# Attention with ropes from SBUF copies, normalisation in the output's evacuation, and transposes one slot later

## The chip, the cores and the metric

The kernel runs on one core of one Trainium2 chip. The metric is the device time of one execution in microseconds (us), the median of several executions. The engines are TensorE (PE in the rows, its weight loads PEld), VectorE (DVE), ScalarE (ACT), GpSimd (POOL) and SyncE (SP), which issues the loads of the weights. SBUF is the on-chip memory that all engines read; PSUM holds TensorE's results.

## What is computed

One layer of a hybrid encoder over 256 tokens of width 2048, with 16 learned meta tokens ahead of them (272 positions). Cut to what matters here:

```python
h = rms_norm(x); aq, ak, av, mk, mq, mv, mo, gates = split(h @ w_in)
# A) differential attention, 8 heads, two components of 64 each
q = rope(aq) * 64 ** -0.5;  k = rope(ak)           # rope on the first 16 of each 64
p = softmax(q @ k.T)                                # for each of two components c
a = p[c=0] - lam * p[c=1]
o_attn = head_rms(a @ av) * gain
# B) bidirectional mLSTM, 4 heads, on mk, mq, mv; gated by sigmoid(mo)
o_ml = head_rms(mlstm(conv(mk), conv(mq), mv)) * gain * sigmoid(mo)
x = x + concat(o_attn, o_ml) @ w_out                # "wo"
x = x + swiglu_ffn(rms_norm(x));  out = rms_norm(x) # gate, up, down
```

## The kernel before, in words

**Stages of TensorE.** Each projection stage computes 512 columns of weights against all tokens: `aq0 ak0 av0 aq1 ak1 av1 mk mq mv0 mv1 mo0 mo1`, then `wo0` to `wo3`, then the FFN. A stage (`project`, L216) has four PSUM accumulators `acc_<stage>_0` to `_3`, and takes the 16 blocks of the inner dimension in 8 pieces of two blocks (`wh_av0_3` is piece 3 of av0). Each product is three matmuls, high by high, high by low, low by high (L251 to L253). The pieces go in pairs: for pieces (0, 1) all four accumulators in turn, 12 matmuls each, then pieces (2, 3), and so on, 48 matmuls for a pair of pieces. A piece's high part is made by ScalarE (`wh`, L205) and its low part by VectorE (`wl`, L206, one instruction for each of the two blocks; in `wo` one for a piece, L213). The PSUM pool holds four accumulators, so the next stage's accumulator j has to wait until this stage's accumulator j has been read.

**Reading the accumulators.** Of aq0 and of av and mv, ScalarE copies each accumulator to an SBUF tile (`value_copy`, L607, `vt_...`, five buffers). Of aq1, ak0 and ak1 the rope itself reads PSUM: a shuffle (L815) and a product (L818) on VectorE, issued with high priority and, but for the first shuffle, pinned to the written order; then a product and a sum on GpSimd (L819, L820).

**Attention** runs beside the projections as a generator that is advanced once for every second piece, a *slot*. For head h and block b of 128 queries, `scores` makes `pss{h}{b}` on TensorE, the row maximum (L860) and its scaling (L861) on VectorE, two exponentials with row sums on ScalarE (L863), then on VectorE the reciprocal (L867), the product with -lambda (L868), the scaled first component (L869) and the difference of both (L870). `transposes` (`pat`, L877) comes one slot after `scores`, `values` (`po`) later, and `finish` writes `om`. `stack` (L829) prepares `qs`, `ks` and `klow` for a head.

**mLSTM.** It runs in the same slots after attention: its last step transposes the normalised heads (`pht{h}{half}`, L804) and ScalarE scales them into `hT` (L807). GpSimd multiplies them with the gate (L977) and subtracts the high part (`split_mix`, L827), which gives `mixh` and `mixl`; `mixh12` to `mixl15` are the last two blocks' worth of pieces, 6 and 7, of `wo`. Behind these GpSimd adds the residual `res` (L990), to which VectorE adds the accumulators of wo (L1000).

**What sets the order.** A scheduler works out one order for each engine ahead of time from the program and its own estimate of times; each engine then runs its list in that order and waits where an operand is late. So an edit in attention moves instructions on all engines, far behind attention too.

Of the kernel before, what the change touches and what calls it, by code (L numbers as in the profile page):

```python
# [86 lines left out]
def tile_hybrid_encoder_layer(  # L87
# [42 lines left out]
    def f(ap):  # L130
        return ap.bitcast(F32)
# [677 lines left out]
    def rope(ps, t0, name, first=False):  # L809
        n = NT - t0  # L810
        dst = kpool.tile([P, n], F32, tag="qk", bufs=32, name=name)
        sh = mp.tile([P, NT], F32, tag="ev", bufs=4, name=f"sh_{name}")
        swap = list(range(8, 16)) + list(range(8)) + list(range(16, 32))
        with tc.high_priority():
            shuffle = V.stream_shuffle(sh[:, :n], ps[:, :n], swap)  # L815
            if not first:
                pin(shuffle)
            pin(V.tensor_tensor(dst, ps[:, :n], ropeC[:, t0:], ALU.mult))  # L818
        G.tensor_tensor(sh[:, :n], sh[:, :n], ropeS[:, t0:], ALU.mult)  # L819
        G.tensor_tensor(dst, dst, sh[:, :n], ALU.add)  # L820
        return dst
# [7 lines left out]
    def attention(h0, nh):  # L829
        es, at, hs, on, qs, ks = {}, {}, {}, {}, {}, {}  # L830

        def stack(h):
            q, k = aq[h], ak[h]
            qs[h] = mp.tile([P, 2, SEQ], F32R, tag="qs", bufs=2, name=f"qs{h}")
            ks[h] = mp.tile([P, 2, NT], F32R, tag="ks", bufs=2, name=f"ks{h}")
            kz = klow[h % 2]
            for c in range(2):
                own, other = slice(64 * c, 64 * c + 64), slice(64 - 64 * c, 128 - 64 * c)
                A.copy(qs[h][own, c, :], q[own])
                A.copy(ks[h][own, c, :], k[own])  # L840
                A.copy(ks[h][other, c, :], k[own])
                V.tensor_tensor(qs[h][other, c, :], q[own], f(qs[h][own, c, :]), ALU.subtract)
                V.tensor_tensor(kz[own, c, :], k[own], f(ks[h][own, c, :]), ALU.subtract)
# [7 lines left out]
        def scores(h, b):  # L851
# [9 lines left out]
            V.tensor_scalar(st[:, 0:2], st[:, 0:2], QK_SCALE, None, ALU.mult)  # L861
            for c in range(2):
                A.activation(  # L863
                    e[:, c, :], pss[:, c, :NT], AF.Exp, bias=st[:, c:c + 1], scale=QK_SCALE,
                    accum_out=st[:, 2 + c:3 + c],
                )
            V.reciprocal(st[:, 4:6], st[:, 2:4])  # L867
            V.tensor_tensor(st[:, 5:6], st[:, 5:6], nlam, ALU.mult)  # L868
            V.tensor_scalar(e[:, 0, :], e[:, 0, :], st[:, 4:5], None, ALU.mult)  # L869
# [13 lines left out]
        def values(h):  # L883
# [10 lines left out]
            A.copy(on[h], po[:, :SEQ].rearrange("p (b d) -> p b d", d=P))  # L894
# [21 lines left out]
        for t in range(n + 3):  # L916
            if t % 2 == 0 and t + 2 < n:
                stack(h0 + t // 2 + 1)
            if t < n:
                scores(h0 + t // 2, t % 2)  # L920
            if 1 <= t <= n:
                transposes(h0 + (t - 1) // 2, (t - 1) % 2)
            if t >= 3 and t % 2:
                values(h0 + (t - 3) // 2)
            if t >= 6 and (t - 6) % 4 == 0:
                finish(h0 + (t - 6) // 2)
                finish(h0 + (t - 6) // 2 + 1)
            if t < n + 2:
                yield
        attending.remove(h0)  # L930

    for g in range(2):
        if g:
            accs = in_proj(C_AQ + N_CHUNK, NM, "aq1")
        if g == 0:
            accs = value_copy(accs, "q0", SEQ)
        for j in range(4):
            aq[4 * g + j] = rope(accs[j], NM, f"aq_{4 * g + j}", g and j == 0)
# [3 lines left out]
        accs = in_proj(C_AK + g * N_CHUNK, 0, f"ak{g}", pre=() if g else pre, pins=0 if g else 4)  # L942
        for j in range(4):
            ak[4 * g + j] = rope(accs[j], 0, f"ak_{4 * g + j}", j == 0)
# [245 lines left out]
```

## Time and profile before

| | |
|---|---|
| median of 3 executions | 1133.64 us (1133.54 to 1134.06) |
| profiled execution | 1134.18 us, of which the span of the engines 1132.3 us |
| TensorE busy | 1114.3 us (98%) |
| VectorE, ScalarE, GpSimd busy | 730.0, 649.6 and 244.5 us |

The span is that of the profiled execution, from its first to its last instruction; 1.9 us of its time lie around it. Busy times add up an engine's instructions. An engine that is 98% busy over the whole span can still wait in a few stages, and these are to be looked for by stretch.

### The profile page before, as it was taken

The page shows a single profiled execution, that of the slowest core. Times are in us where ns is not written, and L with a number is a line of the kernel's source. Part 1 is how long each engine was busy: PE and PEld are TensorE (multiplying, and loading weights), DVE is VectorE, ACT ScalarE, POOL GpSimd, SP SyncE. Part 2 cuts the span into 40 slices and gives each one's busy share as a digit, 9 for nine tenths or more (in the row PEclk, how much of TensorE's full clock was granted, in tenths as well). Part 3 has the DMA queues.
Part 4 walks back from the last instruction along what each step waited for, and adds up shares of the span by engine and source line. Part 5 has one row for each costly group of instructions (what it writes and reads, how often), then busy time and mean ns, then how long its engine had stood idle before and what let it go on. Part 6 is the DMA issues. An engine that isn't in the chain of part 4 may idle for free.

```text
span 1132.3 us, 19840 instructions
## 1 busy us (share of the span) xinstructions
PE 1114.3 (98%) x7629; PEld 1043.5 (92%) x7629; DVE 730.0 (64%) x1153; ACT 649.6 (57%) x1179; POOL 244.5 (22%) x315
## 2 busy tenths in 40 slices
PE   9999999999999999999999999999999999999996
PEld 8889999999999999999999999999999888888896
DVE  6886986998766758566556566556655645454544
ACT  6567688778976445555455555545554644444443
POOL 7320220021045923222122122122122100000000
PEclk9999999999999999999999999999999999999998
DMA  8556446554445666566566576676666765666563
GB/s 258 177 147 185 136 136 181 153 159 142 148 151 185 197 204 194 187 211 199 186 220 190 187 225 191 189 231 189 190 222 189 253 202 200 202 197 203 192 204 109
DMA packets 112255, 212.85 MB, mean 188 GB/s; under 512 B 8906, under 2 KB 9744, under 8 KB 112016
## 3 DMA queue, kind: packets, MB, share of 16 engines
q1 hardware_dynamic: 111664, 210.48, 59.5%
q8 instruction: 60, 0.98, 0.3%
q10 hardware_dynamic: 176, 1.06, 0.3%
q14 instruction: 35, 0.29, 0.1%
q0 software_dynamic: 320, 0.04, 0.0%
HBM read 209.45 MB, written 2.10 MB: 187 GB/s over the span
## 4 chain that ended last, share of the span: by engine, by line
PE 91%; DVE 5%; DMA 2%; issue 1%; ACT 1%; SPq 0%; POOL 0%; ACTq 0%; DVEq 0%; POOLq 0%
PE acc_up L248 14%; PE acc_ga L248 14%; PE acc_ga L249 7%; PE acc_up L249 7%; PE acc_dn L1086 7%; PE acc_dn L1083 7%; PE acc_dn L1087 7%; PE acc_wo L251 3%; PE acc_wo L252 3%; PE acc_wo L253 3%; PE acc_mv L251 1%; PE acc_mv L252 1%; PE acc_mv L253 1%; PE acc_mo L253 1%; PE acc_mo L251 1%; PE acc_mo L252 1%
## 5 line engine op out<-in xcount | busy, mean ns | idle before, releaser
L248 PE MATMUL acc_ga<-vhl,wh_ga 128*128 128x512 f32 x704 | 227.4, 382 | 0.0
L248 PE MATMUL acc_up<-vhl,wh_up 128*128 128x512 f32 x704 | 227.0, 382 | 0.0
L213 DVE TENSOR_TENSOR wl_dn<-raw_dn,wh_dn 128x1024 fp32r<-128x1024 f32 x88 | 108.5, 1234 | 115.5 <-ACT wh_dn L212 115.5
L249 PE MATMUL acc_ga<-vhl,wl_ga 128*128 128x256 f32 x704 | 182.1, 273 | 0.0
L249 PE MATMUL acc_up<-vhl,wl_up 128*128 128x256 f32 x704 | 181.6, 273 | 0.0
L213 DVE TENSOR_TENSOR wl_up<-raw_up,wh_up 128x1024 fp32r<-128x1024 f32 x88 | 114.8, 1335 | 79.8 <-ACT wh_up L212 79.8
L212 ACT CAST wh_dn<-raw_dn 128x1024 fp32r<-128x1024 f32 x88 | 92.3, 1050 | 125.9 <-PE acc_dn L1087 115.8
L213 DVE TENSOR_TENSOR wl_ga<-raw_ga,wh_ga 128x1024 fp32r<-128x1024 f32 x88 | 105.3, 1227 | 68.1 <-ACT wh_ga L212 68.1
L248 PEld LDWEIGHTS acc_ga<-vhl,wh_ga 128*128 128x128 f32 x704 | 130.8, 189 | 16.4
L248 PEld LDWEIGHTS acc_up<-vhl,wh_up 128*128 128x128 f32 x704 | 130.8, 189 | 16.3
L1083 PE MATMUL acc_dn<-wh_dn,ffh 128*128 128x512 f32 (+1 forms) x396 | 141.2, 357 | 0.0
L1087 PE MATMUL acc_dn<-wh_dn,ffl 128*128 128x512 f32 (+1 forms) x396 | 141.2, 357 | 0.0
L1086 PE MATMUL acc_dn<-wl_dn,ffh 128*128 128x512 f32 (+1 forms) x396 | 140.9, 356 | 0.0
L249 PEld LDWEIGHTS acc_up<-vhl,wl_up 128*128 128x128 f32 x704 | 134.1, 192 | 2.3
L249 PEld LDWEIGHTS acc_ga<-vhl,wl_ga 128*128 128x128 f32 x704 | 134.1, 192 | 2.2
L212 ACT CAST wh_ga<-raw_ga 128x1024 fp32r<-128x1024 f32 x88 | 89.1, 1048 | 69.1 <-PE acc_ga L248 34.1
L212 ACT CAST wh_up<-raw_up 128x1024 fp32r<-128x1024 f32 x88 | 88.8, 1047 | 57.0 <-PE acc_ga L248 30.6
L1087 PEld LDWEIGHTS acc_dn<-wh_dn,ffl 128*128 128x128 f32 x396 | 75.1, 190 | 8.2
L1086 PEld LDWEIGHTS acc_dn<-wl_dn,ffh 128*128 128x128 f32 x396 | 75.1, 190 | 8.1
L1083 PEld LDWEIGHTS acc_dn<-wh_dn,ffh 128*128 128x128 f32 x396 | 75.0, 190 | 8.0
L1057 POOL TENSOR_TENSOR sg<-up,sg 128x256 f32<-128x256 f32 x44 | 33.4, 759 | 174.1 <-DVE up L1031 174.0
L252 PE MATMUL acc_wo<-mixl,wh_wo 128*128 128x256 f32 x256 | 70.5, 276 | 0.0
(365 smaller groups left out, 2635.1 us busy)
## 6 DMA issues: line engine op xcount, KB each, us to landing
raw_ga<-in_w_gate_dram SPq DMA_DIRECT2D x88, 512.0 KB, 4.6
raw_up<-in_w_up_dram SPq DMA_DIRECT2D x88, 512.0 KB, 4.6
raw_dn<-in_w_down_dram SPq DMA_DIRECT2D x88, 512.0 KB, 4.6
raw_wo<-in_w_out_dram SPq DMA_DIRECT2D x32, 512.0 KB, 4.2
raw_ak<-in_w_in_dram SPq DMA_DIRECT2D x16, 512.0 KB, 4.1
raw_av<-in_w_in_dram SPq DMA_DIRECT2D x16, 512.0 KB, 4.1
raw_mv<-in_w_in_dram SPq DMA_DIRECT2D x16, 512.0 KB, 4.0
raw_mo<-in_w_in_dram SPq DMA_DIRECT2D x16, 512.0 KB, 4.1
```

Of the source, the lines that this page charges most:

```text
L212: pin(A.copy(wh, raw))
L213: pin(V.tensor_tensor(wl, raw, f(wh), ALU.subtract))
L248: T.matmul(pair, lhsT=qh[:, kk, sl], rhs=both(k), start=first, stop=False)
L249: T.matmul(pair[:, 1], lhsT=ql[:, kk, sl], rhs=xh(k), start=False, stop=last)
L251: T.matmul(o, lhsT=qh[:, kk, sl], rhs=xh(k), start=first, stop=False)
L252: T.matmul(o, lhsT=qh[:, kk, sl], rhs=xl(k), start=False, stop=False)
L253: T.matmul(o, lhsT=ql[:, kk, sl], rhs=xh(k), start=False, stop=last)
L1057: G.tensor_tensor(sgs[j], up, sgs[j], ALU.mult)
L1083: mm = T.matmul(o, lhsT=ffh[:, k, bsl], rhs=ph, start=(k == 0), stop=False)
L1086: T.matmul(o, lhsT=ffh[:, k, bsl], rhs=pl, start=False, stop=False)
L1087: T.matmul(o, lhsT=ffl[:, k, bsl], rhs=ph, start=False, stop=(k == KF - 1))
```

## The change

The scores' scale moves from the exponentials and the maximum to `qs` (ScalarE's copy scales, VectorE's low part becomes one instruction of three operands), so L861 goes. L868 and the second reciprocal product become one instruction that multiplies reciprocal, row sum of the first component and -lambda, and L869 goes: the probabilities stay unnormalised until ScalarE evacuates `po`, in two instructions of 128 columns with the reciprocal as scale, where one copy of 256 columns was. The accumulators of aq1, ak0 and ak1 are copied to SBUF by ScalarE as those of aq0 were; the rope's two VectorE instructions read the copy, without priority or pinning. In the slots `transposes` comes two after `scores` in place of one, `values` and `finish` one slot later, and the generator has one slot more. Behind the edit all line numbers are smaller by 3 or 4.

```diff
--- before.py
+++ after.py
@@ -806,16 +806,13 @@
                 hT[j] = kpool.tile([P, SEQ], F32, tag="qk", bufs=32, name=f"hT{j}")
                 A.activation(hT[j], pht[:, :SEQ], AF.Copy, scale=cols[:, V_MLH + j:V_MLH + j + 1])
 
-    def rope(ps, t0, name, first=False):
+    def rope(ps, t0, name):
         n = NT - t0
         dst = kpool.tile([P, n], F32, tag="qk", bufs=32, name=name)
         sh = mp.tile([P, NT], F32, tag="ev", bufs=4, name=f"sh_{name}")
         swap = list(range(8, 16)) + list(range(8)) + list(range(16, 32))
-        with tc.high_priority():
-            shuffle = V.stream_shuffle(sh[:, :n], ps[:, :n], swap)
-            if not first:
-                pin(shuffle)
-            pin(V.tensor_tensor(dst, ps[:, :n], ropeC[:, t0:], ALU.mult))
+        V.stream_shuffle(sh[:, :n], ps[:, :n], swap)
+        V.tensor_tensor(dst, ps[:, :n], ropeC[:, t0:], ALU.mult)
         G.tensor_tensor(sh[:, :n], sh[:, :n], ropeS[:, t0:], ALU.mult)
         G.tensor_tensor(dst, dst, sh[:, :n], ALU.add)
         return dst
@@ -836,10 +833,12 @@
             kz = klow[h % 2]
             for c in range(2):
                 own, other = slice(64 * c, 64 * c + 64), slice(64 - 64 * c, 128 - 64 * c)
-                A.copy(qs[h][own, c, :], q[own])
+                A.activation(qs[h][own, c, :], q[own], AF.Copy, scale=QK_SCALE)
                 A.copy(ks[h][own, c, :], k[own])
                 A.copy(ks[h][other, c, :], k[own])
-                V.tensor_tensor(qs[h][other, c, :], q[own], f(qs[h][own, c, :]), ALU.subtract)
+                V.scalar_tensor_tensor(
+                    qs[h][other, c, :], q[own], QK_SCALE, f(qs[h][own, c, :]), ALU.mult, ALU.subtract
+                )
                 V.tensor_tensor(kz[own, c, :], k[own], f(ks[h][own, c, :]), ALU.subtract)
 
         def stats(h):
@@ -858,15 +857,12 @@
                 T.matmul(pss[:, c, :NT], lhsT=qs[h][:, c, bsl], rhs=ks[h][:, c, :], start=True, stop=False)
                 T.matmul(pss[:, c, :NT], lhsT=qs[h][:, c, bsl], rhs=klow[h % 2][:, c, :], start=False, stop=True)
             V.tensor_reduce(st[:, 0:2], pss[:, :, :NT], AX.X, ALU.max, negate=True)
-            V.tensor_scalar(st[:, 0:2], st[:, 0:2], QK_SCALE, None, ALU.mult)
             for c in range(2):
                 A.activation(
-                    e[:, c, :], pss[:, c, :NT], AF.Exp, bias=st[:, c:c + 1], scale=QK_SCALE,
-                    accum_out=st[:, 2 + c:3 + c],
+                    e[:, c, :], pss[:, c, :NT], AF.Exp, bias=st[:, c:c + 1], accum_out=st[:, 2 + c:3 + c],
                 )
             V.reciprocal(st[:, 4:6], st[:, 2:4])
-            V.tensor_tensor(st[:, 5:6], st[:, 5:6], nlam, ALU.mult)
-            V.tensor_scalar(e[:, 0, :], e[:, 0, :], st[:, 4:5], None, ALU.mult)
+            V.tensor_scalar(st[:, 5:6], st[:, 5:6], st[:, 2:3], nlam, ALU.mult, ALU.mult)
             V.scalar_tensor_tensor(e[:, 0, :], e[:, 1, :], st[:, 5:6], e[:, 0, :], ALU.mult, ALU.add)
 
         def transposes(h, b):
@@ -891,7 +887,8 @@
                 T.matmul(o, lhsT=atm[h % 2][:, bsl], rhs=val[:, 2, h, :], start=True, stop=False)
                 T.matmul(o, lhsT=at[h][:, 0, bsl], rhs=val[:, 0, h, :], start=False, stop=False)
                 T.matmul(o, lhsT=at[h][:, 1, bsl], rhs=val[:, 1, h, :], start=False, stop=True)
-            A.copy(on[h], po[:, :SEQ].rearrange("p (b d) -> p b d", d=P))
+            for b in range(NB):
+                A.activation(on[h][:, b, :], po[:, b * P:(b + 1) * P], AF.Copy, scale=st[:, b, 4:5])
             for b in range(NB):
                 A.activation(sq[:, b, :], on[h][:, b, :], AF.Square, accum_out=st[:, b, 6:7])
             if h % 2:
@@ -913,35 +910,35 @@
         n = nh * NB
         attending.append(h0)
         stack(h0)
-        for t in range(n + 3):
+        for t in range(n + 4):
             if t % 2 == 0 and t + 2 < n:
                 stack(h0 + t // 2 + 1)
             if t < n:
                 scores(h0 + t // 2, t % 2)
-            if 1 <= t <= n:
-                transposes(h0 + (t - 1) // 2, (t - 1) % 2)
-            if t >= 3 and t % 2:
-                values(h0 + (t - 3) // 2)
-            if t >= 6 and (t - 6) % 4 == 0:
-                finish(h0 + (t - 6) // 2)
-                finish(h0 + (t - 6) // 2 + 1)
-            if t < n + 2:
+            if t >= 4 and t % 2 == 0:
+                values(h0 + (t - 4) // 2)
+            if 2 <= t <= n + 1:
+                transposes(h0 + (t - 2) // 2, (t - 2) % 2)
+            if t >= 7 and (t - 7) % 4 == 0:
+                finish(h0 + (t - 7) // 2)
+                finish(h0 + (t - 7) // 2 + 1)
+            if t < n + 3:
                 yield
         attending.remove(h0)
 
     for g in range(2):
         if g:
             accs = in_proj(C_AQ + N_CHUNK, NM, "aq1")
-        if g == 0:
-            accs = value_copy(accs, "q0", SEQ)
+        accs = value_copy(accs, f"q{g}", SEQ)
         for j in range(4):
-            aq[4 * g + j] = rope(accs[j], NM, f"aq_{4 * g + j}", g and j == 0)
+            aq[4 * g + j] = rope(accs[j], NM, f"aq_{4 * g + j}")
         if g == 0:
             urgent.append(setup())
             urgent.append(gates())
         accs = in_proj(C_AK + g * N_CHUNK, 0, f"ak{g}", pre=() if g else pre, pins=0 if g else 4)
+        accs = value_copy(accs, f"k{g}")
         for j in range(4):
-            ak[4 * g + j] = rope(accs[j], 0, f"ak_{4 * g + j}", j == 0)
+            ak[4 * g + j] = rope(accs[j], 0, f"ak_{4 * g + j}")
         accs = in_proj(C_AV + g * N_CHUNK, 0, f"av{g}")
         vts = value_copy(accs, f"a{g}")
         urgent.append(value_natural(vts, lambda j, g=g: val[:, :, 4 * g + j, :], f"a{g}"))
```

Three places in the orders of the engines show how the instructions move. The first is VectorE in the stage av0, where `sh_ak_j` and `ak_j` are the rope's shuffle and product of accumulator j of ak0, `wl_av0_i` the low part of piece i, `klow` a part of `stack`, and `gnm` and `gnl` gate vectors of the mLSTM. Before:

```order
L815 STREAM_SHUFFLE sh_ak_2_949<-acc_ak0_2_605 128x272
L818 TENSOR_TENSOR ak_2_948<-acc_ak0_2_605,cst_70 128x272
L592 TENSOR_SCALAR gnm_784<-gx_783 64x256
L206 SCALAR_TENSOR_TENSOR wl_av0_2_1039<-raw_av0_2_1036,gm_96,wh_av0_2_1038 128x512
L815 STREAM_SHUFFLE sh_ak_3_955<-acc_ak0_3_606 128x272
L818 TENSOR_TENSOR ak_3_954<-acc_ak0_3_606,cst_70 128x272
L206 SCALAR_TENSOR_TENSOR wl_av0_2_1039<-raw_av0_2_1036,gm_96,wh_av0_2_1038 128x512
L843 TENSOR_TENSOR klow0_553<-ak_0_936,ks0_1255 64x272
L593 TENSOR_TENSOR gnm_784<-gnm_784,gF_782 64x256
L843 TENSOR_TENSOR klow0_553<-ak_0_936,ks0_1255 64x272
L206 SCALAR_TENSOR_TENSOR wl_av0_3_1047<-raw_av0_3_1044,gm_96,wh_av0_3_1046 128x512 x2
```

After:

```order
L814 STREAM_SHUFFLE sh_ak_2_957<-vt_k02_940 128x272
L815 TENSOR_TENSOR ak_2_956<-vt_k02_940,cst_70 128x272
L592 TENSOR_SCALAR gnm_784<-gx_783 64x256
L206 SCALAR_TENSOR_TENSOR wl_av0_2_1047<-raw_av0_2_1044,gm_96,wh_av0_2_1046 128x512 x2
L206 SCALAR_TENSOR_TENSOR wl_av0_3_1055<-raw_av0_3_1052,gm_96,wh_av0_3_1054 128x512
L593 TENSOR_TENSOR gnm_784<-gnm_784,gF_782 64x256
L206 SCALAR_TENSOR_TENSOR wl_av0_3_1055<-raw_av0_3_1052,gm_96,wh_av0_3_1054 128x512
L814 STREAM_SHUFFLE sh_ak_3_963<-vt_k03_942 128x272
L815 TENSOR_TENSOR ak_3_962<-vt_k03_942,cst_70 128x272
L842 TENSOR_TENSOR klow0_553<-ak_0_944,ks0_1263 64x272 x2
L595 TENSOR_TENSOR gnl_545<-gnm_784,gnh_544 64x256
```

The ropes read `vt_k0j`, not the accumulators, and both halves of `wl_av0_3` now stand ahead of the last rope, with the two `klow` behind it.

The second is TensorE at `pat11`, the transposes of head 1, block 1, in stage ak1. Before:

```order
L251 MATMUL acc_ak1_2_1675<-uh_89,wh_ak1_1_1720 128x272
L877 MATMUL pat11_1704<-ident_71,e11_1552 16x128
L879 MATMUL pat11_1704<-ident_71,e11_1552 128x128 x2
L252 MATMUL acc_ak1_2_1675<-ul_90,wh_ak1_1_1720 128x272
L253 MATMUL acc_ak1_2_1675<-uh_89,wl_ak1_1_1721 128x272
L251 MATMUL acc_ak1_3_1676<-uh_89,wh_ak1_0_1712 128x272
```

After:

```order
L251 MATMUL acc_ak1_3_1665<-uh_89,wh_ak1_1_1721 128x272
L252 MATMUL acc_ak1_3_1665<-ul_90,wh_ak1_1_1721 128x272
L253 MATMUL acc_ak1_3_1665<-uh_89,wl_ak1_1_1722 128x272
L857 MATMUL pss21_1776<-ks2_1454,qs2_1453 128x272
L858 MATMUL pss21_1776<-klow0_553,qs2_1453 128x272
L857 MATMUL pss21_1776<-ks2_1454,qs2_1453 128x272
L858 MATMUL pss21_1776<-klow0_553,qs2_1453 128x272
L873 MATMUL pat11_1787<-ident_71,e11_1548 16x128
L875 MATMUL pat11_1787<-ident_71,e11_1548 128x128 x2
L251 MATMUL acc_ak1_0_1662<-uh_89,wh_ak1_2_1795 128x272
```

They stood ten matmuls into `acc_ak1_2` for pieces (0, 1); now they stand behind all four accumulators of these pieces and behind the next scores, `pss21`.

The third is TensorE in wo0. `pht30` and `pht31` are the last transposes of the mLSTM output, from which `mixh14`, `mixh15` and their low parts are made. Before:

```order
L804 MATMUL pht30_4825<-ident_71,hn3_4634 128x128 x2
L252 MATMUL acc_wo0_3_5025<-mixl5_3120,wh_wo0_2_5088 128x256
L253 MATMUL acc_wo0_3_5025<-mixh5_3119,wl_wo0_2_5089 128x256
L804 MATMUL pht31_4830<-ident_71,hn3_4634 128x128 x2
L251 MATMUL acc_wo0_3_5025<-mixh6_3499,wh_wo0_3_5094 128x256
L252 MATMUL acc_wo0_3_5025<-mixl6_3500,wh_wo0_3_5094 128x256
```

After:

```order
L253 MATMUL acc_wo0_2_5024<-mixh10_4621,wl_wo0_5_5155 128x256
L251 MATMUL acc_wo0_2_5024<-mixh11_4626,wh_wo0_5_5154 128x256
L804 MATMUL pht30_4825<-ident_71,hn3_4634 128x128 x2
L252 MATMUL acc_wo0_2_5024<-mixl11_4627,wh_wo0_5_5154 128x256
L804 MATMUL pht31_4830<-ident_71,hn3_4634 128x128 x2
L253 MATMUL acc_wo0_2_5024<-mixh11_4626,wl_wo0_5_5155 128x256
```

They stood in pieces (2, 3), with 92 TensorE instructions of wo0 and the mLSTM ahead of them since the first matmul of wo0, and stand in pieces (4, 5) now, with 144 ahead. The first use of `mixl12` follows in pieces (6, 7). Before, with 153 instructions since the first matmul of wo0 ahead of the row with `mixl12`:

```order
L251 MATMUL acc_wo0_0_5022<-mixh12_4976,wh_wo0_6_5208 128x256
L252 MATMUL acc_wo0_0_5022<-mixl12_4977,wh_wo0_6_5208 128x256
L253 MATMUL acc_wo0_0_5022<-mixh12_4976,wl_wo0_6_5209 128x256
L251 MATMUL acc_wo0_0_5022<-mixh13_4981,wh_wo0_6_5208 128x256
L252 MATMUL acc_wo0_0_5022<-mixl13_4982,wh_wo0_6_5208 128x256
L253 MATMUL acc_wo0_0_5022<-mixh13_4981,wl_wo0_6_5209 128x256
L251 MATMUL acc_wo0_0_5022<-mixh14_4986,wh_wo0_7_5214 128x256
L252 MATMUL acc_wo0_0_5022<-mixl14_4987,wh_wo0_7_5214 128x256
```

After, with 166 ahead:

```order
L251 MATMUL acc_wo0_0_5022<-mixh12_4976,wh_wo0_6_5208 128x256
L251 MATMUL acc_wo0_1_5023<-mixh12_4976,wh_wo0_6_5208 128x256
L251 MATMUL acc_wo0_2_5024<-mixh12_4976,wh_wo0_6_5208 128x256
L251 MATMUL acc_wo0_3_5025<-mixh12_4976,wh_wo0_6_5208 128x256
L252 MATMUL acc_wo0_0_5022<-mixl12_4977,wh_wo0_6_5208 128x256
L253 MATMUL acc_wo0_0_5022<-mixh12_4976,wl_wo0_6_5209 128x256
L251 MATMUL acc_wo0_0_5022<-mixh13_4981,wh_wo0_6_5208 128x256
L252 MATMUL acc_wo0_1_5023<-mixl12_4977,wh_wo0_6_5208 128x256
```

Where accumulator 0 ran through all of its last 12 matmuls before, the four accumulators now take turns, so that all four end close to the end of wo0.

## Rows read from the trace of the kernel before

**Rows 1.** Windows of 50 us: length, then busy us (and instructions) of each engine, clock, DMA.
```profile
50.00:100.00 50.00, 47.17 (x397) 45.72 (x396) 38.41 (x74) 31.40 (x60) 7.95 (x8) 1.00 0.63 188
100.00:150.00 50.00, 48.73 (x424) 48.26 (x422) 43.31 (x106) 38.21 (x108) 8.93 (x11) 1.00 0.51 145
150.00:200.00 50.00, 48.16 (x415) 47.93 (x416) 38.05 (x83) 40.45 (x102) 7.84 (x19) 1.00 0.52 152
200.00:250.00 50.00, 50.00 (x442) 49.98 (x442) 46.00 (x124) 36.71 (x99) 5.46 (x9) 1.00 0.54 158
```

**Rows 2.** Waits of TensorE over the span: engine line, waited for, us, times, longest.
```profile
PE pat L877 <- DVE e L870: 3.0, 2, 1.8
PE acc_av L251 <- DVE ak L818: 2.0, 1, 2.0
...
PE acc_av L253 <- DVE wl_av L206: 0.4, 1, 0.4
PE pct L602 <- ACT gnm L596: 0.4, 1, 0.4
```

**Rows 3.** Timeline of TensorE in av0: start, us, engine line op, operands, count.
```profile
66.47 0.28 PE L253 MATMUL acc_av<-uh,wl_av 128*128 128x272 f32 x1
...
67.63 0.28 PE L251 MATMUL acc_av<-uh,wh_av 128*128 128x272 f32 x1
```

**Rows 4.** Timeline of VectorE in av0.
```profile
73.21 1.00 DVE L843 TENSOR_TENSOR klow<-ak,ks 64x272 fp32r<-64x272 f32 x1
...
76.08 1.41 DVE L206 SCALAR_TENSOR_TENSOR wl_av<-raw_av,gm,wh_av 128x512 fp32r<-128x512 f32 x2
```

**Rows 5.** Timeline of ScalarE at the end of ak0.
```profile
65.22 1.33 ACT L205 ACTIVATE wh_av<-raw_av,gm 128x512 fp32r<-128x512 f32 x2 [2.02 <-PE acc_ak L252]
```

**Rows 6.** Groups of instructions by line and shape.
```profile
L869 DVE TENSOR_SCALAR e<-e,hs 128x272 f32<-128x272 f32 x16 | 6.8, 425 | 0.0
...
L894 ACT COPY on<-po 128x256 f32<-128x256 f32 x8 | 2.8, 356 | 0.0
```

**Rows 7.** The same view from 36 to 180 us: the rope's product.
```profile
L818 DVE TENSOR_TENSOR ak<-acc_ak,cst 128x272 f32<-128x272 f32 x8 | 3.4, 430 | 0.1
L818 DVE TENSOR_TENSOR aq<-vt_q,cst 128x256 f32<-128x256 f32 x4 | 2.3, 568 | 0.0
```

**Rows 8.** Timeline of TensorE at `pat11`.
```profile
123.88 0.28 PE L251 MATMUL acc_ak<-uh,wh_ak 128*128 128x272 f32 x1
125.35 0.28 PE L877 MATMUL pat<-ident,e 128*16 128x128 f32 x1 [1.19 <-DVE e L870]
```

**Rows 9.** Timeline of VectorE ahead of `pat11`.
```profile
121.67 0.91 DVE L869 TENSOR_SCALAR e<-e,hs 128x272 f32<-128x272 f32 x1
...
124.33 0.96 DVE L870 SCALAR_TENSOR_TENSOR e<-e,hs 128x272 f32<-128x272 f32 x1
```

**Rows 10.** Timeline of VectorE ahead of `pat31`.
```profile
147.57 1.87 DVE L842 TENSOR_TENSOR qs<-aq,qs 64x256 fp32r<-64x256 f32 x2
...
153.26 0.99 DVE L870 SCALAR_TENSOR_TENSOR e<-e,hs 128x272 f32<-128x272 f32 x1
```

**Rows 11.** Timeline of TensorE in wo0: its first matmul, `pht30`, the first use of `mixl12`.
```profile
343.01 0.28 PE L251 MATMUL acc_wo<-mixh,wh_wo 128*128 128x256 f32 x1
...
353.27 0.38 PE L804 MATMUL pht<-ident,hn 128*128 128x128 f32 x2
...
360.07 0.28 PE L252 MATMUL acc_wo<-mixl,wh_wo 128*128 128x256 f32 x1
```

**Rows 12.** Timeline of GpSimd in wo0.
```profile
354.31 0.74 POOL L977 TENSOR_TENSOR sgm<-sgm,hT 128x256 f32<-128x256 f32 x1 [1.06 <-ACT hT L807]
...
356.92 3.87 POOL L827 TENSOR_TENSOR mixl<-sgm,mixh 128x256 fp32r<-128x256 f32 x4
360.87 12.54 POOL L990 TENSOR_TENSOR res<-uh,ul 128x256 f32<-128x256 f32 x10
```

**Rows 13.** Timeline of VectorE in wo0.
```profile
356.85 1.23 DVE L213 TENSOR_TENSOR wl_wo<-raw_wo,wh_wo 128x1024 fp32r<-128x1024 f32 x1 [0.48 <-ACT wh_wo L212]
```

## The prediction

> **What bounds the kernel now.** I read the windows first, since the change touches only a few stages: TensorE waits nowhere from 200 us on (50.00 of 50 from 200 to 250, and so in each window up to 400), and falls short of 50 by 2.8, 1.3 and 1.8 us in the three windows from 50 to 200 [rows 1]. So whatever the change takes off VectorE or ScalarE, it can win back a few microseconds at most, and only where TensorE waits. The clock is full there, 1.00. Then the waits of TensorE [rows 2], to see who ends them: `pat` behind the probabilities `e` of VectorE, 3.0 us in two waits; `acc_av` behind the rope's product `ak`, 2.0; `wl_av` 0.4; `pct` 0.4. What is left of the list lies in the first 36 us, which the change leaves as they are. VectorE is the one that is late: 38 to 43 us busy of 50 [rows 1], with its instructions queued where TensorE waits.
>
> A wait's row leaves out the restart. At `pat11` the row says 1.19, but from the matmul ahead of it (123.88) to it (125.35) it is 1.47, and matmuls of this width follow each other every 0.116 (ten intervals from 66.47 to 67.63 [rows 3]); so it costs 1.36, 0.17 more than the row [rows 8]. By that the two waits of `pat` cost 3.0 + 2 x 0.17 = 3.3, and the three in av0 2.8 + 3 x 0.17 = 3.3. That is all there is to win: 6.6.
>
> **The change, part by part.**
>
> *The waits at `pat11` and `pat31`: -3.3.* At `pat11`, VectorE's queue held, among ropes and weights, the 0.91 of L869, which goes, ahead of `e`, which ran from 124.33 to 125.3 [rows 9]. In the new order `pat11` stands fourteen matmuls of `acc_ak1_2` and `_3` and four of `pss21` later, some 2.1 us, so its need moves to 126.1 or later, counted from where the wait was. Counting VectorE's new list, without L869 and with `e` ahead of the last ropes, `e11` ends near 122.5. For it to wait again VectorE would have to be over 3.5 us late. `pat31` is alike: `e` started at 153.26 behind the two `qs` of 1.87 and L869 [rows 10], and the new place of `pat31` is another slot on; I put `e31` near 148 and the need near 153. L869 goes 16 times, 425 ns each [rows 6], 6.8 us of VectorE in all; behind 200 us this lies beside a busy TensorE and is worth nothing. Bounds: nothing below -3.4, and -2.8 if ScalarE's copies of ak1 (next part) cost av1 half a microsecond.
>
> *The copies.* Twelve copies go to ScalarE. The nearest row is a copy of 256 columns out of PSUM, 356 ns [rows 6]; ScalarE sits idle 2.02 us right ahead of 65.22, at the end of ak0 [rows 5], which covers the four copies of ak0 (1.4) nearly in full. If that cover were gone, each would cost av0 0.36. In aq1 and ak1 ScalarE is 38 of 50 busy [rows 1], and accumulators 1 to 3 come 1.4 us apart (12 x 0.116), so the copies keep up; I take 0 to 0.5, entered as 0.1.
>
> *The rope's wait in av0: -1.0.* The accumulators of ak0 now come free with ScalarE's copies, so the 2.0 (with restart 2.2) of `acc_av` goes. But VectorE's work stays, and the next thing it owes TensorE is `wl_av0_3`. Before, its second half ended at 76.08 + 1.41 = 77.5 [rows 4]. In the new order the last rope (a shuffle and a product of 0.43, together 0.9) and two `klow` of some 1.0 and 0.9 [rows 4, 7] stand behind it: 77.5 - 0.9 - 1.9 = 74.7. TensorE wants it as the 12th matmul of pieces (2, 3): av0 starts at 66.24 (two intervals ahead of 66.47 [rows 3]), 48 matmuls take 5.57, and eleven more 1.28: 73.1. So a new wait of 1.6 with bounds of 1.1 and 2.0, by how much GpSimd slows the ropes. `wl_av0_5` is late next: VectorE does one rope, four `klow`, `gnl` and four `wl` of 0.7 in the 5.6 us of TensorE's next pair, 5.6 to 6.9 by how they overlap; I take the middle, a wait of 0.65, with 0 and 1.3 as ends. Left in av0: 2.25 and two restarts, 2.6, for 3.3 now; the `pct` wait was partly the same lateness and goes along, another 0.3. So -1.0, with ends of -2.0 and +0.3.
>
> Here the trace and a rule pull apart. The rope's product takes 430 ns from PSUM, and 568 where it reads an SBUF copy, on fewer columns (256 for 272), with GpSimd's part of the rope beside it [rows 7]: +0.14 for each, and more in single ones. The Trainium skill, "SBUF — State Buffer", section "SBUF: two separate sides", says that a VectorE instruction with two SBUF inputs and a GpSimd one that reads SBUF exclude each other, and that the loser fully blocks; the PSUM source of before is outside that rule, and the copies bring twelve products under it. By rows it costs 0.14 x 3 ahead of `wl_av0_3`, inside my bounds; by the rule it could be a GpSimd instruction's length each, which is a rival below.
>
> *The evacuation of `po`.* Two scaled copies for one of 356 ns [rows 6]: at most 0.36 more, eight times, on ScalarE. `on` is needed a slot or more later, so 0; with that cover gone each costs 0.36 once. The folded scale takes a small instruction out of the way from maximum to exponentials; no TensorE wait hangs on it: 0.
>
> *One slot later: the end of attention and the mLSTM: +0.2.* The extra slot is taken from room at the end of each group of heads, but the mLSTM starts behind it, and its pieces stand about a slot (two pieces, 5.4 us) later in TensorE's order up to wo0. I find slack at nearly all of them; `pht00` in mo1 has next to none: 0 to 1.0, entered as 0.1, and 0.1 for the copies above.
>
> *wo0 and wo1: +2.65.* This is where the change pays. Before, GpSimd ended the four `mixl` at 356.92 + 3.87 = 360.8, the first of them well ahead of its use at 360.07 [rows 11, 12]. TensorE's instructions there follow each other every 0.1115 (153 between 343.01 and 360.07 [rows 11]). `pht30` had 92 instructions ahead of it (353.27) and now has 144: 52 x 0.1115 = 5.8 later. `mixl12` was wanted after 153 and is wanted after 166: only 1.45 later, 361.5 on the old clock. From `pht30` at 359.1, ScalarE's last `hT` is there some 1.5 later as I count its list, and then GpSimd needs one product (0.74 alone [rows 12]) and the subtraction: about 362.3. That is a wait of some 0.85 if nothing collides. But the four subtractions took 3.87, 0.97 each, for 0.74 alone, and the first ran over VectorE's `wl_wo` of 1.23 [rows 12, 13]. With 1.2 us of each turn of 12 matmuls (1.34) against up to 1.8 for a subtraction that collides, two collisions cost 0.5 each: 1.85. Then, as all four accumulators now end together at the end of wo0, `acc_wo1_0` waits for VectorE's residual sum, and this for GpSimd's `res`, which starts only behind the last `mixl` and took 1.25 each (12.54 for ten [rows 12]): 0.8 more. Ends: 0.85 without collision, and 3.7 if a piece of weights on ScalarE (about 1 us) gets ahead of the last `hT`.
>
> **Sum.** -3.3 - 1.0 + 0.2 + 2.65 = -1.45. Against the profiled execution's 1134.18 (span 1132.3 and 1.9 around it) that is 1132.7; it lay 0.54 above the median of the runs shown, so 1132.2 for the median. From this kernel's spread I take 0.2% (2.3 us) as what can be told from no change; the forecast is inside it.
>
> **The rivals.**
>
> *The late mLSTM is covered.* If the last `mixl` meets no VectorE instruction and `res` keeps up, wo0 costs 0 to 0.85, and what was won stays: -3.3 - 1.0 + 0.1 + 0.4 = -3.8, 1129.8 (1128.9 to 1131). For it: GpSimd's own work is short. Against it: 5.8 us later with 1.45 of room, counted from the orders. 0.27.
>
> *Slower: VectorE and GpSimd block each other fully.* Each rope's product then waits for a GpSimd instruction of 0.74 in place of 0.14 more, +0.6 for three ropes, +1.8 in av0 and some 0.6 for the fourth; and in wo0/wo1 each subtraction and `res` pays a `wl_wo` of 1.23, 4.8 in place of 2.65. -3.3 + 1.4 + 0.2 + 4.8 = +3.1: 1136.7. It decides once a block costs over 0.5 us each time. For it: subtractions at 0.97 and ropes at 568 are means, so single ones pay far more. Against it: in these rows most meet for part of their length only. This is what the rule named above would give, and the rows bear it out in part. 0.16.
>
> *The change does not do what it says.* ScalarE, with twelve copies and sixteen evacuations more, becomes the late one in ak1 and av1: the copies of ak1 stand behind exponentials, each accumulator of av1 waits 0.36, and the two waits at `pat` come back as 1.4 to 2 there: about -0.2, 1133.4. Against it: ScalarE is the less busy engine in each of these windows but one [rows 1]. 0.13.
>
> The forecast itself has the remaining 0.44, with a range of its own of 1130.8 to 1133.9. All of the first rival and a quarter of the forecast's cases are faster by over 0.2% (below 1131.4): 0.38. Slower (above 1135.9) is most of the second rival: 0.13. Same: 0.49. The range from 1129.2 to 1135.6 leaves out the ends of both.
>
> **What would show it.** In the waits of TensorE: no `pat` at 123.9 and 152.3 (else the first part is wrong); at av0 no wait for `ak`, but one of 1 to 2 us behind `wl_av` near 73; a wait of `acc_wo` L252 behind GpSimd's `mixl` and one of `acc_wo` behind `res` near 360 to 366, 2.65 in all. TensorE's busy time in the windows 50 to 200 rises by 4 to 5 us, and that from 350 to 400 falls. The prediction is wrong if the mLSTM's last pieces arrive in time, or if a wait stands in aq1 to mv1 behind ScalarE.

## The result, and the profile after

The changed kernel took 1136.47 us (median of 12, 1135.53 to 1137.28) against 1133.72 for the kernel before (12 runs, 1133.16 to 1135.25): ratio 1.0023, 95% interval 1.0015 to 1.0031. It is slower by 2.75 us, where 1132.2 was forecast, with a range of 1129.2 to 1135.6.

The page of the changed kernel, its span and the busy times:

```profile
span 1134.2 us, 19813 instructions
...
PE 1116.1 (98%) x7629; PEld 1044.6 (92%) x7629; DVE 730.9 (64%) x1121; ACT 654.9 (58%) x1199; POOL 245.9 (22%) x315
```

VectorE has 32 instructions fewer and is busy as long as before. TensorE's waits, in the columns of [rows 2]:

```profile
PE pct L602 <- ACT gnm L596: 3.4, 1, 3.4
...
PE acc_wo L252 <- POOL mixl L824: 0.6, 1, 0.6
...
PE pss L857 <- ACT e L861: 0.5, 1, 0.5
PE acc_av L253 <- DVE wl_av L206: 0.4, 1, 0.4
PE acc_wo L251 <- DVE res L997: 0.3, 1, 0.3
```

Both waits of `pat` and the wait for `ak` of [rows 2] are gone, as forecast. The waits in wo are there, as forecast. What was not forecast is the first row: `pct`, 0.4 before, now waits 3.4 for one exponential of ScalarE. The windows that answer to [rows 1], and that from 350 to 400:

```profile
50.00:100.00 50.00, 46.14 (x368) 44.47 (x366) 36.38 (x66) 30.89 (x61) 10.27 (x8) 0.93 0.59 173
100.00:150.00 50.00, 49.55 (x434) 49.23 (x433) 42.93 (x101) 41.35 (x116) 7.70 (x9) 1.00 0.54 153
150.00:200.00 50.00, 50.00 (x434) 49.87 (x433) 39.69 (x74) 41.49 (x109) 11.22 (x21) 1.00 0.53 158
...
350.00:400.00 50.00, 48.89 (x431) 48.12 (x430) 34.34 (x36) 25.65 (x38) 42.19 (x39) 1.00 0.58 182
```

From 100 to 200 TensorE's busy time rose by 2.7 us. From 50 to 100 it fell by 1.0, with 29 instructions fewer (397 before), and the granted clock fell to 0.93. So from 50 to 200 it rose by 1.6, where 4 to 5 was forecast. To see the sum by stage, I took the time from the first matmul of a stage to the first of a later one, in this kernel and in all the runs below (us):

```
               av0    aq1..av1  mk..mo  wo0..wo3  FFN
before         27.51  83.94     165.43  86.63     693.87
after          30.94  80.98     164.26  90.01     693.87
ak1_sum_v      28.47  80.90     164.26  90.01     693.87
exp_first      27.29  80.91     164.27  90.02     693.87
mixl_v         31.91  80.93     164.27  88.98     693.87
slots_before   31.60  80.47     165.44  86.63     693.86
gap            31.97  80.92     164.24  90.03     693.87
both           27.29  80.46     165.44  86.63     693.86
b_copies       31.11  83.45     165.44  86.63     693.87
a_psum         27.51  83.27     164.25  90.00     693.87
gap_long       31.46  80.91     164.26  90.01     693.86
both_gem       29.29  80.48     165.44  86.63     693.87
b_norm         27.93  80.51     165.42  86.63     693.87
gap_shuffle    26.94  80.91     164.27  90.02     693.87
```

A stage whose orders are the same takes the same time within 0.1 us from kernel to kernel, which makes this the sharpest measure here; av0 alone varies, with the clock (below). What the table leaves out is the time ahead of av0: av0 starts between 65.04 and 66.45 us in these profiles, so that two executions can lie over 1 us apart before the change counts. The change gave +3.43 in av0, -2.96 in aq1 to av1, and +2.21 from mk to wo3 together (ten matmuls of `pnum31`, 1.1 us, only moved from mo1 to wo0). That is +2.68, for +2.75 in the medians.

**What happened in av0.** VectorE's timeline there:

```profile
70.48 2.06 DVE L206 SCALAR_TENSOR_TENSOR wl_av<-raw_av,gm,wh_av 128x512 fp32r<-128x512 f32 x3
72.47 0.41 DVE L593 TENSOR_TENSOR gnm<-gnm,gF 64x256 f32<-64x256 f32 x1
72.80 0.73 DVE L206 SCALAR_TENSOR_TENSOR wl_av<-raw_av,gm,wh_av 128x512 fp32r<-128x512 f32 x1
73.47 0.00 DVE L814 LOAD_MASK_SELECT sh_ak<-vt_k  x1
73.47 0.45 DVE L814 STREAM_SHUFFLE sh_ak<-vt_k 128x272 f32<-128x272 f32 x1
73.82 0.76 DVE L815 TENSOR_TENSOR ak<-vt_k,cst 128x272 f32<-128x272 f32 x1
```

GpSimd's in the same stretch, the last sum of the rope of `ak_1` and that of `ak_3`:

```profile
70.37 3.91 POOL L817 TENSOR_TENSOR ak<-ak,sh_ak 128x272 f32<-128x272 f32 x1
...
76.20 0.84 POOL L817 TENSOR_TENSOR ak<-ak,sh_ak 128x272 f32<-128x272 f32 x1
```

ScalarE's, which has the casts of head 1 (`ks`, from `ak_1`) ahead of the gates' exponential in its list:

```profile
74.31 0.42 ACT L837 CAST ks<-ak 64x272 fp32r<-64x272 f32 x1 [3.32 <-POOL ak L817]
...
76.06 1.28 ACT L596 ACT_TABLE_LOAD   x1
77.35 0.42 ACT L596 ACTIVATE gnm<-gnm 64x256 f32<-64x256 f32 x1
```

And TensorE's, and its clock in windows of 2 us (columns as above):

```profile
77.82 0.36 PE L602 MATMUL pct<-ident,gnm 64*128 64x64 f32 x1 [3.38 <-ACT gnm L596]
...
78.72 0.43 PE L253 MATMUL acc_av<-uh,wl_av 128*128 128x272 f32 x1
78.94 0.43 PE L251 MATMUL acc_av<-uh,wh_av 128*128 128x272 f32 x1
```

```profile
74.00:76.00 2.00, 0.44 (x4) 0.24 (x3) 1.97 (x3) 1.62 (x4) 2.00 (x3) 0.85 0.83 227
76.00:78.00 2.00, 0.18 (x2) 0.18 (x3) 1.94 (x4) 1.97 (x4) 0.96 (x2) 0.50 0.62 231
78.00:80.00 2.00, 2.00 (x10) 1.88 (x10) 1.72 (x4) 2.00 (x4) 0.00 (x0) 0.50 0.00 1
...
82.00:84.00 2.00, 2.00 (x18) 2.00 (x18) 0.00 (x0) 0.53 (x1) 0.00 (x0) 0.94 0.96 284
```

Read from the bottom up: TensorE waits for an exponential whose input was ready at 72.9. ScalarE had not got to it, since the casts ahead of it waited 3.32 us for `ak_1`; the four casts, and the 1.28 us of ACT_TABLE_LOAD ahead of the exponential, stand there as before. GpSimd needed 3.91 us for a sum that took 0.84 for `ak_3` at 76.20, while VectorE ran five instructions with two SBUF inputs each without a break. The sum ended 0.8 us after the shuffle, which reads one operand, had started. And once TensorE had stood still, its clock was granted at half (1.2 GHz): matmuls follow each other after 0.22 us (78.72 to 78.94) in place of 0.116 until about 82.

### The profile page after: what moved, and what is told of

Its sections match the earlier page's. It is cut to its first block, busy times and chain, and to the rows that moved or that the text cites. A ratio compares the mean times of both kernels' runs of the same rounds, so it can differ in the third digit from the quotient of the medians.

```text
span 1134.2 us, 19813 instructions
## 1 busy us (share of the span) xinstructions
PE 1116.1 (98%) x7629; PEld 1044.6 (92%) x7629; DVE 730.9 (64%) x1121; ACT 654.9 (58%) x1199; POOL 245.9 (22%) x315
## 4 chain that ended last, share of the span: by engine, by line
PE 92%; DVE 3%; DMA 1%; POOL 1%; ACT 1%; issue 1%; SPq 0%; ACTq 0%; POOLq 0%
PE acc_ga L248 14%; PE acc_up L248 14%; PE acc_up L249 7%; PE acc_ga L249 7%; PE acc_dn L1080 7%; PE acc_dn L1084 7%; PE acc_dn L1083 7%; PE acc_wo L251 2%; PE acc_wo L252 2%; PE acc_wo L253 2%; PE acc_mv L252 1%; PE acc_mv L251 1%; PE acc_mv L253 1%; PE acc_mo L252 1%; PE acc_mo L251 1%; PE acc_mo L253 1%
```

## The experiments

**ak1_sum_v.** One instruction moves to another engine:

```diff
-        G.tensor_tensor(dst, dst, sh[:, :n], ALU.add)
+        (V if name == "ak_1" else G).tensor_tensor(dst, dst, sh[:, :n], ALU.add)
```

> The changed kernel with one instruction moved: the last sum of the rope of ak_1 (L817) runs on VectorE in place of GpSimd; every other engine's order stays. Theory A, GpSimd blocked: in the changed kernel this sum took 3.9 us for 0.8 because VectorE ran five instructions with two SBUF inputs back to back beside it, and ScalarE's list, then the exponential of the gates, then pct on TensorE waited for it. Then the wait of pct falls from 3.4 to under 0.6 us, the granted clock stays 1.00 from 76 to 82 us, av0 is 3 to 4.5 us shorter, and the time falls by about 4 us, to 1132.5. Rival B, VectorE is simply behind: the sum adds 0.4 us to its list, ak_1 is as late, and the wait of pct stays over 2 us; the time changes by less than 0.7 us.

Measured: 1133.26 us (1131.32 to 1134.58), ratio to before 0.9993 (0.9985 to 1.0002): 3.2 us less than the changed kernel, av0 28.47. That is 2.5 us off av0, where 3 to 4.5 was expected: the wait of `pct` fell to 1.0, not under 0.6, and the clock still fell, for a shorter time. Giving VectorE more work shortened the stage, which its lateness cannot explain. And the block did not go, it hit the next sum, `ak_2`, on which nothing of av0 hangs yet. GpSimd's timeline:

```profile
71.56 4.16 POOL L817 TENSOR_TENSOR ak<-ak,sh_ak 128x272 f32<-128x272 f32 x1
```

**exp_first.** The exponential goes ahead of the casts of head 1 in ScalarE's list:

```diff
-        A.activation(gem, gem, AF.Exp)
+        gem_exp.append(A.activation(gem, gem, AF.Exp))
...
-                A.copy(ks[h][own, c, :], k[own])
-                A.copy(ks[h][other, c, :], k[own])
+                with tc.issue_after(gem_exp[0].ins) if h == 1 else ExitStack():
+                    A.copy(ks[h][own, c, :], k[own])
+                    A.copy(ks[h][other, c, :], k[own])
```

> The changed kernel with the exponential of the gates (L596) put ahead of head 1's four casts (ks1) in ScalarE's list; TensorE's pct stands eleven matmuls earlier by that. Theory A needs both links, the blocked sum and a list that is run in order: with the exponential ahead of the casts the sum of ak_1 still takes 3 to 4 us, but pct waits under 1 us, the clock stays 1.00 and the time falls by 3 to 4.5 us. Rival B: the exponential's own input is late on VectorE, pct waits 2 us or more, the time changes by less than 1 us.

Measured: 1132.59 us (1131.76 to 1133.40), ratio 0.9989 (0.9980 to 0.9998), 3.9 us less than the changed kernel; av0 27.29, clock 1.00. The sum of `ak_1` still took 3.91. `pct` waits 1.5, more than expected, since it stands eleven matmuls (1.3 us) earlier and the exponential's own input, L593, ended only at 72.5. So both links are needed, the blocked sum and the list run in order behind it.

**gap, gap_long, gap_shuffle.** One instruction more on VectorE, between the halves of `wl_av0_2`, that writes a tile nothing reads; no order changes otherwise. In gap and gap_long it sets 1 and 512 columns, in gap_shuffle it shuffles 272 columns of `ones` (here gap_shuffle's; the tile's allocation and the order for the second half of `wl_av0_2` are left out):

```diff
+                if name == "av0_2" and kk == 0:
+                    last = nc.cur_bb.bb.instructions[-1]
+                    with tc.issue_after(last):
+                        gap.append(V.stream_shuffle(gapt[:, :NT], ones, list(range(32))))
```

> The changed kernel with one more instruction: VectorE sets one column of a tile that nothing reads, between the two halves of wl_av0_2; no other order changes. Theory A in its sharper form: GpSimd's sum of ak_1 is held off as long as VectorE's instructions with two SBUF inputs follow each other without a break, five of them from 70.5 to 73.5 us. Then the break lets it through: it ends some 2 us earlier (1.5 to 2.5 us long in place of 3.9), the wait of pct falls from 3.4 by about 2 us, and with less of the slow clock the time falls by 2 to 4 us, though work was added. Rival, that an instruction merely waits out the VectorE instruction that runs when it starts, or is slow by sharing: the sum stays at 3.5 us or more, the time is unchanged.

> As the run with the one column, but VectorE sets 512 columns there, some 0.3 to 0.6 us. In the runs so far the blocked sum always ended 0.8 us after the start of VectorE's next shuffle, which reads one SBUF operand for 0.45 us, and the break of 0.06 us let nothing through. If a break lets GpSimd in once it is long enough, the sum of ak_1 ends within 1 us of this break's start (2 us long at most), the wait of pct falls from 3.4 by 1 us or more, and the time falls by 1.5 to 4 us. If the break is not what matters, but the shuffle or the last rope itself, the sum still takes 3.9 us or more and the time is the changed kernel's or up to 0.6 us above it.

> As the two runs with a break, but the instruction between the halves of wl_av0_2 is a shuffle of 272 columns, as the rope's, from one SBUF tile into a tile that nothing reads. Setting columns did not let GpSimd's sum through, neither one column (0.06 us) nor 512 (0.48 us). If what lets it in is a VectorE instruction that reads at most one SBUF operand, as the rope's shuffle seemed to, the sum of ak_1 ends some 0.8 us after this shuffle's start, so it is under 2 us long; the wait of pct falls from 3.4 to 1.5 to 2.3, and the time falls by 1.5 to 3.5 us though VectorE has more to do. If the sum still takes 3.5 us or more, what lets GpSimd in stays open, and the time is the changed kernel's or up to 0.6 us more.

Measured: gap 1136.59 us (1135.08 to 1138.00; 1.0026, 1.0015 to 1.0037), the sum 3.92 us long; gap_long 1136.73 us (1135.42 to 1137.52; 1.0026, 1.0016 to 1.0036), the sum 3.62:

```profile
71.02 3.92 POOL L825 TENSOR_TENSOR ak<-ak,sh_ak 128x272 f32<-128x272 f32 x1
```

```profile
70.33 3.62 POOL L825 TENSOR_TENSOR ak<-ak,sh_ak 128x272 f32<-128x272 f32 x1
```

gap went as its rival said. gap_long lies between: the time is the rival's, but the sum took 3.62 where it said 3.9 or more, and `pct` waits 2.1 in place of 3.4, as the theory said; `wl_av`, behind the added work, now waits 1.4 in place of 0.4, so nothing is won. Setting columns, for 0.06 or 0.48 us, did not let the sum through while it ran, and my first wording, that any break does, is wrong.

gap_shuffle: 1132.71 us (1131.77 to 1133.56; 0.9993, 0.9984 to 1.0002), 3.8 us less than the changed kernel by one useless instruction (1.5 to 3.5 was expected). VectorE and GpSimd in it:

```profile
71.53 0.45 DVE L224 STREAM_SHUFFLE gapt<-ones 128x272 f32<-128x272 f32 x1
71.88 2.06 DVE L206 SCALAR_TENSOR_TENSOR wl_av<-raw_av,gm,wh_av 128x512 fp32r<-128x512 f32 x2
```

```profile
70.75 1.47 POOL L825 TENSOR_TENSOR ak<-ak,sh_ak 128x272 f32<-128x272 f32 x1
```

The sum ends 0.69 us after the shuffle's start, and now it is VectorE that is held: its next two `wl`, 1.41 for a pair in [rows 4], take 2.06. `pct` no longer waits (1.5 to 2.3 was expected); `wl_av` does, 1.5 in three waits. The clock stays 1.00, and av0 is 26.94, shorter than in any other run.

**mixl_v.** The last four subtractions on VectorE:

```diff
-        G.tensor_tensor(mixl[k], apart(src), f(mixh[k]), ALU.subtract)
+        (V if k >= 12 else G).tensor_tensor(mixl[k], apart(src), f(mixh[k]), ALU.subtract)
```

> The changed kernel with the four subtractions for mixl12 to mixl15 on VectorE in place of GpSimd. If GpSimd's late list is what TensorE waits for in wo0 and wo1 (four gaps of 0.78, 0.25, 0.25 and 0.5 us, 1.8 in all), the waits for mixl go, res starts some 3 us earlier, and the time falls by 1.2 to 1.8 us. If the late step is ScalarE's mixh or the transposes pht themselves, the waits stay under another name and the time changes by less than 0.5 us.

Measured: 1135.74 us (1134.43 to 1136.57; 1.0015, 1.0006 to 1.0024), 0.7 less; wo0 to wo3 1.03 shorter, for 1.2 to 1.8 expected. Two gaps stay, 0.46 behind `mixl` and 0.3 behind `res`. So GpSimd's late list is about half of the loss in wo. The rest goes with the later slot, as slots_before shows; that it is the lateness of the transposes themselves is argued, not shown.

**slots_before.** Attention's slots as they were (`transposes` one slot after the scores, n + 3 slots); the rest of the change stays:

```diff
-        for t in range(n + 4):
+        for t in range(n + 3):
...
-            if 2 <= t <= n + 1:
-                transposes(h0 + (t - 2) // 2, (t - 2) % 2)
+            if 1 <= t <= n:
+                transposes(h0 + (t - 1) // 2, (t - 1) % 2)
...
```

> The changed kernel with the slots of attention as before (transposes one slot after the scores, one slot fewer); the ropes' copies, the folded scale and the normalisation in the evacuation stay. If it was the later slot that cleared the two waits at pat, they come back with some 3.3 us and the gaps in wo0 and wo1 (1.8 and what follows, 2.2) go: plus 1 us, 1137.5. If it was VectorE's shorter list with the ropes unpinned, the pats still do not wait, and only the gaps in wo go: minus 2 us, 1134.4. The wait of pct in av0 stays 3.4 in both.

Measured: 1133.76 us (1133.02 to 1134.68; 1.0001, 0.9993 to 1.0010), 2.7 less than the changed kernel. wo0 to wo3 is back at 86.63, and no `pat` waits: aq1 to av1 takes 80.47, even less than with the later slot. The later slot won nothing here and cost 2.2 in mk to wo3 and 0.5 in aq1 to av1.

**a_psum, b_copies, b_norm.** Parts of the change alone: a_psum is the changed kernel with the ropes of before (from PSUM, with priority and pins); b_copies is the kernel before with only the ropes' copies; b_norm is the kernel before with only the folded scale and the normalisation in the evacuation. The edits are the pieces of the diff above.

> The changed kernel with the ropes of aq1, ak0 and ak1 as before, from PSUM, with priority and pins; scale, normalisation and the later slot stay. If the loss in av0 is the copies' doing, av0 is 27.5 us again with its waits for ak (2.0) and pct (0.4), and the clock stays full: minus 3.4 against the changed kernel. The gaps in wo stay, 2.2. With the waits at pat cleared by the later slot the time is 1132.5 to 1133; with one of them back, 1134.

> The kernel before with the ropes' copies alone (no priority and no pins, no other part of the change). If the loss in av0 is the copies' doing, it is all there: wait of pct 3.4 us, slow clock, av0 near 31 us in place of 27.5, plus 3.4. The waits at pat tell whether the ropes that were pinned ahead of the probabilities caused them: gone, minus 3.3, so the time stays near 1133.7; still there, 1137. wo0 has no gaps, since the slots are as before.

> The kernel before with the folded scale and the normalisation in the evacuation alone (ropes from PSUM with pins, slots as before). av0 as before, 27.5 us with full clock, and no gaps in wo0. If VectorE's shorter list is enough for the probabilities, the two waits at pat (3.3 us) go: 1130.3. If the pinned ropes ahead of them are the cause, waits of some 2 to 3 us stay in ak1 and av1: 1133 to 1134.

Measured: a_psum 1135.66 us (1134.37 to 1136.22; 1.0017, 1.0008 to 1.0026), over what either case gave; b_copies 1136.74 (1136.37 to 1137.67; 1.0030, 1.0019 to 1.0040); b_norm 1130.23 (1129.54 to 1130.81; 0.9969, 0.9957 to 0.9980). av0 is 27.51 in a_psum and 31.11 in b_copies: its loss comes with the new ropes and with no other part of the change. Both runs exchange the source of the ropes together with their priority and pins, so which of these took the pauses out of VectorE's list is not shown. What I had expected wrongly of a_psum is in its waits:

```profile
PE acc_av L251 <- DVE ak L818: 2.0, 1, 2.0
PE pss L860 <- ACT e L864: 1.4, 1, 1.4
...
PE pat L876 <- ACT on L894: 1.1, 1, 1.1
```

With pinned ropes and the later slot, two waits of the old size stand in ak1, one at the scores and one at `pat`, in a new guise. b_copies has such a pair as well (`pss` 1.5, `pat` 1.2, behind ScalarE), and with it its 1137 came out, not its 1133.7. In b_norm one wait of 0.2 is left at `pat`: the folded scale and the missing L869 clear them by themselves, with pinned ropes and the slots of before. The later slot, which is all that a_psum adds to b_norm, brings waits back there (aq1 to av1 83.27 for 80.51).

One expectation of b_norm failed: its av0 is 27.93, not 27.5 at full clock. Behind the same wait of 2.0 for `ak` that the kernel before and a_psum have, its clock was granted at half (0.50 from 70 to 72 us, 1.00 there in both others).

**both and both_gem.** The changed kernel with the slots of before and the exponential ahead of the casts; both_gem puts L593 ahead of `wl_av0_2` and `wl_av0_3` too.

```diff
+                with tc.issue_after(gem_sub[0].ins) if name == "av0_2" else ExitStack():
                     split_scaled(wh[:, kk, :], wl[:, kk, :], raw[:, kk, :], gain[:, k0 + kk:k0 + kk + 1], pin)
```

> The changed kernel with the slots as before and the exponential of the gates ahead of head 1's casts. If the two losses found so far are apart from each other, the gains add: minus 2.7 and minus 3.9 against the changed kernel, so 1129.9 (1129.2 to 1131), with av0 near 27.3 us, wo0 to wo3 near 86.6 us, and no wait at pat. If one gives back the other, it stays above 1131.5.

> The kernel with the earlier slots and the exponential ahead of the casts, and the gates' subtraction (L593) put ahead of wl_av0_2 and wl_av0_3 on VectorE. If the 1.5 us that pct still waits there is that subtraction, two microseconds of wl ahead of it, the wait falls to 0.2 to 0.6 and av0 from 27.3 to 26.3: 1128.9 (1128.3 to 1129.6). If VectorE's total is what counts in av0, wl_av0_2 and wl_av0_3 come 0.4 us later and take it back: 1129.5 to 1130.2.

Measured: both 1129.85 us (1129.14 to 1130.64; 0.9967, 0.9955 to 0.9980), as expected: the two losses add. both_gem 1130.52 (1129.64 to 1131.68; 0.9973, 0.9963 to 0.9984): `pct` no longer waits, but `wl_av` does, 1.7 in three waits, and the clock falls behind them to 0.57 from 82 to 86 us; av0 is 29.29 for 27.29. This was the rival's way, and worse than it said.

## Why the prediction was wrong, step by step

**The waits at `pat`: -3.3.** Right in size: aq1 to av1 got shorter by 2.96, with a new wait of 0.6 (0.5 and the restart) at `pss` within it. The reason was half right. I rested it on `pat11` standing 18 matmuls later; slots_before and b_norm show that VectorE's shorter list does it without that, and a_psum that the later place does not do it where the ropes are pinned.

**The rope's wait in av0: -1.0, measured +3.43.** This is the step that failed, in the sentence "the `pct` wait was partly the same lateness and goes along, another 0.3". I followed VectorE's list to its debts to TensorE (`wl_av0_3`, `wl_av0_5`), and these stayed small: the gaps there are 0.2, 0.2, 0.55 and 0.27, 1.2 for the 2.25 forecast. (That av0 starts at 66.24 was misread by 0.1, it is 66.13; this changes nothing.) But I did not follow GpSimd's sum, which the same list holds up, nor ScalarE's list behind it. The waits in av0 (the gaps between matmuls) add up to 4.8 for 3.5 before, so some 1.3 of the 3.43 are waits. Of the other 2.1 the half clock, which the sum had not at all, has most: 17 intervals between matmuls of about 0.22 us in place of 0.116, 1.85 more in all.

**The contention.** I priced it as time that VectorE's ropes lose (0.14 each), and in the rival of the full block as 0.6 each, again mostly on VectorE; that rival's 1136.7 is near the measured time, but not by this sum. The price fell on GpSimd: 3.1 us for one sum. The Trainium skill, "SBUF — State Buffer", section "SBUF: two separate sides", says that a VectorE instruction with two SBUF inputs and a GpSimd one that reads SBUF exclude each other and that the loser fully blocks. The trace agrees: in gap_shuffle first the sum is held by `wl`, then `wl` by the sum. The Trainium skill also says there that whichever starts first gets the ports for the whole instruction. The traces leave this open: the sum is recorded from 70.37, 0.11 ahead of VectorE's `wl` at 70.48, and was held through five instructions, not one; in both_gem, where it is recorded 0.22 ahead of the next instruction with two SBUF inputs, it went through in 0.82, and that instruction, L593, took 0.88 for 0.41. Before, the ropes of PSUM stood between the `wl` and let the same sum through in 1.48 us. VectorE and GpSimd before:

```profile
71.17 0.74 DVE L206 SCALAR_TENSOR_TENSOR wl_av<-raw_av,gm,wh_av 128x512 fp32r<-128x512 f32 x1
71.84 0.00 DVE L815 LOAD_MASK_SELECT sh_ak<-acc_ak  x1
71.84 0.46 DVE L815 STREAM_SHUFFLE sh_ak<-acc_ak 128x272 f32<-128x272 f32 x1
72.21 0.41 DVE L818 TENSOR_TENSOR ak<-acc_ak,cst 128x272 f32<-128x272 f32 x1
```

```profile
71.06 1.48 POOL L820 TENSOR_TENSOR ak<-ak,sh_ak 128x272 f32<-128x272 f32 x1
```

That spacing is what the copies and the new order removed.

**One slot later, and wo.** Forecast +0.2 and +2.65, measured +2.21 together. The mechanism was right. The terms: the waits for `mixl` came to 1.3 (0.78, 0.25 and 0.25) for 1.85, and that for `res` to 0.5 for 0.8. GpSimd in wo, after:

```profile
360.15 4.82 POOL L824 TENSOR_TENSOR mixl<-sgm,mixh 128x256 fp32r<-128x256 f32 x4
365.04 9.57 POOL L987 TENSOR_TENSOR res<-uh,ul 128x256 f32<-128x256 f32 x10
```

The four subtractions took 4.82 (3.87 in [rows 12]), with two that collided, as the sum had it.

**The copies, +0.1.** ScalarE kept up: no wait of TensorE is for a copy of an accumulator. The kernels with copies have a wait of 0.6 at `plam` in ak0, behind VectorE, which those with the old ropes do not have, and ak0 takes 28.65 for 28.46. The wait of 0.6 at `pss` in ak1, behind ScalarE, is not the copies' alone: slots_before has them too, and no such wait.

With av0 as measured and the wait at `pss`, the steps of the sum give -3.3 + 0.6 + 3.4 + 2.2 = +2.9, for the 2.75 of the medians.

What stays open: why setting columns lets nothing through and a shuffle does; and in gap_long the sum got in after L593, which reads two operands, before the next shuffle. A LOAD_MASK_SELECT stands ahead of every shuffle in these lists, and no run tells it from the shuffle. The runs show what let the sum in here, not the rule. Open too is when the clock falls: the wait of 2.0 in av0 was followed by half clock in b_norm, and not in a_psum or in the kernel before.

## What to carry to other kernels

When an edit takes pauses out of VectorE's list (here the ropes' shuffles and products from PSUM, among instructions with two SBUF inputs), look at what GpSimd has to do in that stretch and who waits for it in order, rather than at VectorE's own debts alone. A wait of TensorE of 3.4 us cost another 1.85 to 2.9 us here, as the clock was granted at half behind it. An edit of several parts is best costed part by part in the runs: one part here is worth -3.4 alone (b_norm), another +3.1 alone (b_copies), and the later slot costs 2.7 on top of both (slots_before).

## What the runs showed of the hardware that was not expected

A GpSimd sum of 0.84 us took 3.9 while VectorE's two-input instructions followed each other, and one useless shuffle of 0.45 us on VectorE made the kernel 3.8 us faster. The half clock cost differently much in kernels with the same waits in av0, 4.8 us each: 17, 25 and 26 intervals between matmuls at about 0.22 us in the changed kernel, mixl_v and gap, and av0 30.94, 31.91 and 31.97. In the changed kernel the clock had fallen by 75.5, 2.3 us before TensorE went on at 77.82, so part of the half clock passed while TensorE stood; in the others it fell only 0.4 and 0.3 us before TensorE went on. What sets that moment is not shown.
